# Last quarter of a squared-ReLU MLP: w_down's last 1,024 rows as a plain feature-major product instead of in seven products

## The chip, the cores and the metric

One core of one Trainium2 chip runs the whole decoder trunk (one layer, batch 1, 512 tokens, model width 1,024). The metric is the device time of one execution in microseconds, the median over repeated runs. Everything is in float32; the matmul operands are written as two float32r halves (a high half and the remainder), and each product is made of three matmuls.

## The reference, cut to what matters

```python
for i in range(DEPTH):                       # DEPTH = 1
    ...
    x = x + y @ w_out[i]                     # x1 in the kernel
    h2 = rms_norm(x, norm_mlp[i])
    x = x + jnp.square(jax.nn.relu(h2 @ w_up[i])) @ w_down[i]     # x2 in the kernel
    ple_gate = jax.nn.sigmoid(rms_norm(x, norm_ple[i]) @ w_ple_gate[i])
    x = x + ple_gate * (p[i] @ w_ple[i])
```

x is 512 x 1,024, w_up 1,024 x 4,096, w_down 4,096 x 1,024, w_ple_gate 1,024 x 1,024, p 512 x 256, w_ple 256 x 1,024. What comes ahead of `x @ w_out` (gated linear attention, block attention, their branches) is the same before and after the change.

## The kernel before, in words

**Layout.** Activations lie feature-major: 128 features on the partitions, 512 tokens along the free axis, 8 such tiles for the model width (KT = 8). A feature-major product (`gemm_fm`) takes one weight block of 1,024 x 128 (8 pieces of 128 x 128 as the stationary operand) and lets 128 x 512 tiles of the activation stream past; `mm3` issues the three matmuls of a pair of halves (lines 102, 103 and 104), so that one block is 24 matmuls of 512 columns into one of two PSUM banks ("acc").

**Order.** TensorE's order is written out by the program. `tick` is called twice per block: after 12 and after 24 matmuls. It first runs what was planned for this tick with `at(t, f)`, then advances small generators (`spawn`) by a step. A block's evacuation (`evac`) is issued behind its second tick, and what it spawns goes on with the next tick. Each engine then works through its own queue in this order and waits by semaphores.

**Weights.** A 512 KB weight block is loaded by SP's queue into one of three `raw` buffers 7 ticks ahead of its use (`unit`), and 3 ticks ahead `make` has it split: ScalarE writes the high half (`whi`, line 162), VectorE the remainder (`wlo`, line 164).

**The MLP.** It is cut into four quarters of 1,024 hidden features. In quarter g, eight blocks U0 to U7 form relu(h2 @ w_up) in feature-major tiles, which are then squared (`F`, slot a0). The product with w_down's 1,024 x 1,024 quarter is formed token-major by a scheme of seven half-size products P1 to P7 instead of eight (`quarter`): tokens, features and outputs are halved, sums and differences of `F` (GpSimd and VectorE) and of the weights (accumulating DMAs, `down_units`) are the operands, each product is 24 matmuls into two banks ("aux"), and `subtotal` and GpSimd add the results into `acc` (slot a6, 512 x 1,024, tokens on the partitions). The table `blocks` fixes the order: U0 to U3 of a quarter lie between the products of the quarter before, so that the last quarter has U4, U5, U6, P5, U7, P1, P2, P6, P7, P3, P4. `TP` is the tick at which the table ends.

**Turning back and the end.** `acc` is token-major and x2 is needed feature-major. `turn_back(i0)` transposes two feature tiles (four 128 x 128 transposes each, line 1012, into one bank), VectorE adds x1 to them (line 1018; x1 was written to DRAM as `spill` and is read back into slot a4 by `back_x1`), splits them for the next product (lines 97 and 98) and squares and sums them for the norm. Two of its four calls lie at the last two ticks of the table, two in the first p @ w_ple product (`gemm_ple(ple0)`: 4 tiles of 6 matmuls, evacuated by ScalarE in line 1078 from the two "acc" banks). Then come the norm's two matmuls (line 385), the eight gate blocks (`ple_gate`) and the other half of p @ w_ple (`ple1`, `ple_last`), which multiplies, adds and writes the result out.

```python
at(TP - 2, lambda: turn_back(0))
at(TP - 1, lambda: turn_back(2))
...
back = [4, 6]                    # gemm_ple: turn_back(back.pop(0)) behind every second tile
```

Of the kernel before, what the change touches and what calls it, by code (L numbers as in the profile page):

```python
# [21 lines left out]
F32 = mybir.dt.float32  # L22
# [22 lines left out]

@with_exitstack
def kernel(ctx: ExitStack, tc: tile.TileContext, xT, pT, w_in, w_val, w_glr, w2, cols,
                      w_a, w_b, w_out, w_up, w_down, w_gate, w_ple, outT):
    nc = tc.nc
    const = ctx.enter_context(tc.tile_pool(name="const", bufs=1))  # L50
    big = ctx.enter_context(tc.tile_pool(name="big", bufs=1))
# [9 lines left out]
    def nm(s):  # L61
        uid[0] += 1
        return f"{s}_{uid[0]}"
# [4 lines left out]
    def slot(tag, shape, dt=F32):  # L68
        return big.tile(shape, dt, tag=tag, name=nm(tag))
# [5 lines left out]
    def tt(tag, dt=F32):  # L75
        return tmp.tile([P, T], dt, tag=tag, name=nm(tag), bufs=BUFS.get(tag, 2))

    def bank(pool=auxp, tag="aux"):
        return pool.tile([P, T], F32, tag=tag, name=nm(tag))
# [37 lines left out]
    def at(t, f):  # L117

        plan.setdefault(t, []).append(f)
# [141 lines left out]
    def make(raw):  # L261
        hi = wp.tile([P] + list(raw.shape[1:]), F32R, tag="whi", name=nm("whi"))
        lo = wp.tile([P] + list(raw.shape[1:]), F32R, tag="wlo", name=nm("wlo"))
        ready.append((hi, lo))
        jobs.insert(0, [halves(hi, lo, raw), 0])

    blocks = [("U", 0, j) for j in range(4)]
    for g in range(4):  # L270
        mix = ["U4", "U5", "U6", "P5", "U7", "P1", "P2", "P6", "n0", "P7", "n1", "P3", "n2", "P4", "n3"]
        for z in mix:
            k = int(z[1])
            if z[0] != "n":
                blocks.append((z[0], g, k))
            elif g < 3:
                blocks.append(("U", g + 1, k))
    start = {z: T0 + 2 * j for j, z in enumerate(blocks)}
    TP = T0 + 2 * len(blocks)

    def down_units(g):


        c = {k: start["P", g, k] for k in range(1, 8)}
        box = {}

        def load(t, name, tag, u, src):
            def f():
                if name not in box:
                    box[name] = slot(tag, [P, 2, 512] if tag[0] == "v" else [P, 2, 2, 512])  # L290
                nc.sync.dma_start(out=of(name, u), in_=src)
            at(t, f)

        def of(name, u):
            return box[name] if name[0] == "S" else box[name][:, u]

        def add(t, name, u, src):
            at(t, lambda: G.dma_start(out=of(name, u), in_=src, accum_op=ALU.add))

        def use(k, name, u):  # L300
            at(c[k] + u - 3, lambda: make(of(name, u)))

        for u in range(2):
            a11, a12 = w_down[0, 4 * g + u], w_down[0, 4 * g + 2 + u]
            a21, a22 = w_down[1, 4 * g + u], w_down[1, 4 * g + 2 + u]
            t = c[5] + u
            S = f"S{u}"
            load(t - 10, S, f"v{u}", u, a22)
            load(t - 9, "A21", "c0", u, a21)
            load(t - 8, "A11", "c1", u, a11)  # L310
            load(t - 1, "A12", "c3", u, a12)
            load(c[1] + u, "A22", "c1", u, a22)
            add(t - 8, S, u, a21)
            add(t - 5, "A21", u, a11)
            add(t - 1, S, u, a11)
            if g < 3:
                add(c[6] + u - 1, S, u, a12)
            else:
                last_sum(t, u, (a22, a21, a11, a12))
            for k, name in ((5, S), (1, "A11"), (6, S), (2, "A12"), (7, "A21"), (3, S), (4, "A22")):  # L320
                if g < 3 or k != 3:
                    use(k, name, u)
                else:
                    at(c[3] + u - 3, lambda u=u: make(sums[u]))

    sums = {}

    def last_sum(t, u, srcs):

        def f():  # L330
            sums[u] = wp.tile([P, 2, 512], F32, tag="raw", name=nm("raw"))
            nc.sync.dma_start(out=sums[u], in_=srcs[0])
        at(start["U", 3, 7] + u - 6, f)
        for j in range(3):
            at(start["U", 3, 7] + u + 3 * j - 4, lambda j=j: G.dma_start(out=sums[u], in_=srcs[j + 1],
                                                                     accum_op=ALU.add))

    for g in range(4):
        for j in range(8):
            unit(start["U", g, j], w_up[8 * g + j, 0])  # L340
        down_units(g)
    unit(TP, w_ple[0])
    for j in range(8):
        unit(TP + 2 + 2 * j, w_gate[j, 0])
# [518 lines left out]

    acc = None
    h3 = []
    s2 = R2 = x2 = p_hl = None

    def subtotal(first, out, ps, op):

# [133 lines left out]

        return block

    def turn_back(i0):

        nonlocal s2, R2
        for i in range(i0, i0 + 2):
            ps = bank()  # L1010
            for m in range(NT):
                PE.transpose(ps[:, m * P:(m + 1) * P], acc[:, m, i * P:(i + 1) * P], ident)
            if not i:
                h3.append(slot("a5", [P, KT, T], F32R))
                h3.append(slot("a0", [P, KT, T], F32R))
                R2 = const.tile([P, T], F32, tag="R", name="R2")
                s2 = tt("s")
            V.tensor_tensor(x2[:, i], ps, x2[:, i], ALU.add)
            scaled_split(h3[0][:, i], h3[1][:, i], x2[:, i], col[:, C_PLE + i:C_PLE + i + 1])
            if i == 0:  # L1020
                A.activation(s2, x2[:, i], AF.Square)
            else:
                q = tt("q2")
                A.activation(q, x2[:, i], AF.Square)
                G.tensor_tensor(s2, s2, q, ALU.add)
            if i == KT - 1:
                spawn(norm_end(R2, s2), 1)

    def back_x1():
        nonlocal x2  # L1030
        x2 = slot("a4", [P, KT, T])
        nc.sync.dma_start(out=x2, in_=spill)

    def load_p():
        nonlocal p_hl
        raw = wp.tile([P, 2, T], F32, tag="raw", name=nm("raw"))
        nc.sync.dma_start(out=raw, in_=pT)
        yield 1
        p_hl = slot("c0", [P, 4, T], F32R)
        yield from halves(p_hl[:, :2], p_hl[:, 2:], raw)  # L1040

    at(start["P", 3, 1] + 1, back_x1)
    at(start["P", 3, 3], lambda: spawn(load_p()))
    at(TP - 2, lambda: turn_back(0))
    at(TP - 1, lambda: turn_back(2))
    quarters = {}
    for z, g, i in blocks:
        if g not in quarters:
            quarters[g] = quarter(g)
        quarters[g](z, i)  # L1050


    mid = slot("a1", [P, KT, T])

    back = [4, 6]

    def gemm_ple(evac, n=4):
        w = ready.pop(0)
        for i in range(n):
            ps = bank(accp, "acc")  # L1060
            ms = slice(i * P, (i + 1) * P)
            for k in range(2):
                mm3(ps, (w[0][:, k, ms], w[1][:, k, ms]), (p_hl[:, k], p_hl[:, 2 + k]), k == 0, k == 1)
            if i == 3:
                convert()
            if i % 2:
                if back:
                    turn_back(back.pop(0))
                tick()
            evac(i, ps)  # L1070
        return w

    def finish(i, e):
        V.tensor_tensor(e, e, x2[:, i], ALU.add)
        nc.sync.dma_start(out=outT[i * P:(i + 1) * P], in_=e)

    def ple0(i, ps):
# [1 line left out]

    def ple_gate(i, ps):  # L1080
        e = tt("e") if i < 4 else mid[:, i]
        if i < 2:
            A.activation(e, ps, AF.Copy)
        else:
            V.tensor_tensor(e, ps, R2, ALU.mult)
            A.activation(e, e, AF.Sigmoid)

        def rest():
            if i < 2:
                yield 2 - i  # L1090
                V.tensor_tensor(e, e, R2, ALU.mult)
                A.activation(e, e, AF.Sigmoid)
                yield 1
            V.tensor_tensor(e, e, mid[:, i], ALU.mult)
            finish(i, e)
            yield 1
        if i < 4:
            spawn(rest())

    def ple1(i, ps):  # L1100
        e = mid[:, 4 + i]
# [3 lines left out]
    def ple_last(w):  # L1105

        for c in range(2):
            s = slice(c * 256, (c + 1) * 256)
            ps = bank(accp, "acc")
            ms = slice(3 * P, 4 * P)  # L1110
            for k in range(2):
                mm3(ps[:, :256], (w[0][:, k, ms], w[1][:, k, ms]), (p_hl[:, k, s], p_hl[:, 2 + k, s]),
                    k == 0, k == 1)
            e = mid[:, KT - 1, s]
            V.tensor_tensor(e, e, ps[:, :256], ALU.mult)
            V.tensor_tensor(e, e, x2[:, KT - 1, s], ALU.add)
            nc.sync.dma_start(out=outT[(KT - 1) * P:, s], in_=e)

    gemm_ple(ple0)
# [66 lines left out]
```

## Time and profile before

| | us |
|---|---|
| median of 3 runs (lowest to highest) | 976.58 (975.85 to 977.4) |
| the profiled execution, its own time | 977.64 |
| its span, first to last instruction | 975.9 |
| TensorE busy (98% of the span) | 956.2 |
| VectorE busy (63%) | 619.1 |
| ScalarE busy (48%) | 470.1 |
| GpSimd busy (24%) | 232.3 |

How to read it: PE is TensorE, PEld its weight loads, DVE VectorE, ACT ScalarE, POOL GpSimd, SP the engine that issues most DMAs. A matmul's record is longer than the time until the next one starts, since matmuls are pipelined; what a matmul costs in a stream is the distance from start to start. The clock is TensorE's granted clock as a share of full speed (1.00 is 2.4 GHz, 0.50 is 1.2 GHz). The execution's own time is 1.7 us above its span.

### The profile page before, as it was taken

The page shows a single profiled execution, that of the slowest core. Times are in us where ns is not written, and L with a number is a line of the kernel's source. Part 1 is how long each engine was busy: PE and PEld are TensorE (multiplying, and loading weights), DVE is VectorE, ACT ScalarE, POOL GpSimd, SP SyncE. Part 2 cuts the span into 40 slices and gives each one's busy share as a digit, 9 for nine tenths or more (in the row PEclk, how much of TensorE's full clock was granted, in tenths as well). Part 3 has the DMA queues.
Part 4 walks back from the last instruction along what each step waited for, and adds up shares of the span by engine and source line. Part 5 has one row for each costly group of instructions (what it writes and reads, how often), then busy time and mean ns, then how long its engine had stood idle before and what let it go on. Part 6 is the DMA issues. An engine that isn't in the chain of part 4 may idle for free.

```text
span 975.9 us, 11466 instructions
## 1 busy us (share of the span) xinstructions
PE 956.2 (98%) x4360; PEld 791.7 (81%) x4360; DVE 619.1 (63%) x807; ACT 470.1 (48%) x691; POOL 232.3 (24%) x204
## 2 busy tenths in 40 slices
PE   9999999999999999999999999999999999999698
PEld 7888888878888888888888888788878878887486
DVE  5469989785556763333365555775695596589564
ACT  4558878774155842212323354624443353353551
POOL 0027674610321000000000004142153334335300
PEclk9999999999999999999999999999999999999799
DMA  7222121213211232343223459528635852994041
GB/s 259 86 87 66 64 77 46 74 58 108 87 65 45 74 121 87 108 150 130 87 99 109 139 183 269 134 83 242 189 88 175 215 149 79 310 276 133 22 151 43
DMA packets 34903, 121.15 MB, mean 124 GB/s; under 512 B 4000, under 2 KB 4384, under 8 KB 34464
## 3 DMA queue, kind: packets, MB, share of 16 engines
q1 hardware_dynamic: 29520, 101.53, 29.9%
q0 software_dynamic: 5184, 18.88, 10.1%
q8 instruction: 34, 0.56, 0.2%
q14 instruction: 21, 0.17, 0.0%
q10 hardware_dynamic: 144, 0.02, 0.0%
HBM read 116.21 MB, written 4.19 MB: 123 GB/s over the span
## 4 chain that ended last, share of the span: by engine, by line
PE 85%; DVE 9%; ACT 3%; issue 2%; POOL 0%; DVEq 0%; ACTq 0%; POOLq 0%
PE acc L102 22%; PE acc L104 22%; PE acc L103 22%; PE aux L103 5%; PE aux L104 5%; PE aux L102 5%; DVE wlo L164 3%; DVE a L164 2%; DVE a L871 1%; ACT whi L162 1%; PE aux L583 1%; PE aux L750 1%; PE aux L386 1%; PE aux L385 1%; PE aux L753 1%
## 5 line engine op out<-in xcount | busy, mean ns | idle before, releaser
L102 PE MATMUL acc<-a,whi 128*128 128x512 f32 x832 | 326.4, 392 | 0.0
L104 PE MATMUL acc<-a,wlo 128*128 128x512 f32 x832 | 324.5, 390 | 1.6 <-DVE wlo L164 1.6
L103 PE MATMUL acc<-a,whi 128*128 128x512 f32 x832 | 324.3, 390 | 0.0
L164 DVE TENSOR_TENSOR wlo<-raw,whi 128x1024 fp32r<-128x1024 f32 x130 | 172.7, 1331 | 95.8 <-ACT whi L162 94.6
L162 ACT ACTIVATE whi<-raw 128x1024 fp32r<-128x1024 f32 x130 | 136.4, 1050 | 108.1 <-PE acc L103 71.3
L104 PEld LDWEIGHTS acc<-a,wlo 128*128 128x128 f32 x832 | 156.3, 188 | 35.9 <-DVE wlo L164 2.8
L102 PEld LDWEIGHTS acc<-a,whi 128*128 128x128 f32 x832 | 156.5, 188 | 32.1
L103 PEld LDWEIGHTS acc<-a,whi 128*128 128x128 f32 x832 | 156.5, 188 | 31.8
L103 PE MATMUL aux<-wlo,a 128*128 128x512 f32 x288 | 112.3, 390 | 1.5 <-DVE wlo L164 1.5
L104 PE MATMUL aux<-whi,a 128*128 128x512 f32 x288 | 112.6, 391 | 0.0
L102 PE MATMUL aux<-whi,a 128*128 128x512 f32 x288 | 112.2, 390 | 0.0
L936 POOL TENSOR_TENSOR c<-a 128x256 f32<-128x256 f32 x16 | 14.1, 885 | 315.3 <-ACT a L925 315.3
L103 PEld LDWEIGHTS aux<-wlo,a 128*128 128x128 f32 x288 | 54.1, 188 | 13.6 <-DVE wlo L164 2.4
L104 PEld LDWEIGHTS aux<-whi,a 128*128 128x128 f32 x288 | 54.1, 188 | 12.6 <-DVE a L164 1.5
L102 PEld LDWEIGHTS aux<-whi,a 128*128 128x128 f32 x288 | 54.1, 188 | 11.1
L925 ACT ACTIVATE a<-a 128x512 f32<-128x512 f32 x32 | 20.1, 630 | 71.9 <-DVE a L917 68.6
L164 DVE TENSOR_TENSOR wlo<-c,whi 128x1024 fp32r<-128x1024 f32 x32 | 48.8, 1555 | 8.7 <-ACT whi L162 8.7
L162 ACT ACTIVATE whi<-c 128x1024 fp32r<-128x1024 f32 x32 | 33.7, 1055 | 31.4 <-PE acc L103 12.4
L513 POOL TENSOR_TENSOR ql<-q,qh 128x512 fp32r<-128x512 f32 x16 | 22.9, 1430 | 86.3 <-ACT qh L511 86.3
L102 PE MATMUL acc<-c,whi 128*128 128x512 f32 (+1 forms) x82 | 32.9, 402 | 7.2 <-ACT a L1078 7.1
L810 ACT ACTIVATE a<-a 128x512 f32<-128x512 f32 x16 | 10.1, 632 | 61.5 <-DVE a L809 61.5
L871 DVE TENSOR_TENSOR a<-a,aux 128x512 f32<-128x512 f32 x42 | 27.1, 681 | 17.0 <-PE aux L104 17.0
(211 smaller groups left out, 1362.0 us busy)
## 6 DMA issues: line engine op xcount, KB each, us to landing
raw<-in_w_in_dram SPq DMA_DIRECT2D x48, 512.0 KB, 3.2
raw<-in_w_up_dram SPq DMA_DIRECT2D x32, 512.0 KB, 3.7
c<-in_w_down_dram SPq DMA_DIRECT2D x32, 512.0 KB, 10.1
v<-in_w_down_dram POOLq DMA_DIRECT2D x22, 512.0 KB, 9.0
raw<-in_w_val_dram SPq DMA_DIRECT2D x14, 512.0 KB, 3.3
raw<-in_w_a_dram SPq DMA_DIRECT2D x8, 512.0 KB, 3.2
raw<-in_w_b_dram SPq DMA_DIRECT2D x8, 512.0 KB, 3.2
raw<-in_w_out_dram SPq DMA_DIRECT2D x8, 512.0 KB, 3.4
```

The lines of the kernel that those rows point to most:

```text
L102: PE.matmul(ps, a[0], b[0], start=start, stop=False)
L103: PE.matmul(ps, a[0], b[1], start=False, stop=False)
L104: PE.matmul(ps, a[1], b[0], start=False, stop=stop)
L162: A.activation(hi, src, AF.Copy)
L164: (eng or V).tensor_tensor(lo, src, f32(hi), ALU.subtract)
L385: PE.matmul(ps, ones[n], sh, start=True, stop=False)
L386: PE.matmul(ps, ones[n], sl, start=False, stop=True)
L513: G.tensor_tensor(sl, q2, f32(sh), ALU.subtract)
L810: A.activation(s, s, AF.Sigmoid)
L871: V.tensor_tensor(out, out, ps, op)
L925: A.activation(e, e, AF.Square)
L936: G.tensor_tensor(t1[:, k], F[:, 0, i], F[:, 1, i], ALU.subtract)
```

## The change

The last quarter's eight products of w_up are followed by eight blocks W0 to W7: a plain feature-major product of all 1,024 squared features with one 1,024 x 128 column block of w_down's last quarter, which the host lays out as `w_last`. The sums that the seven products needed (of features, of weights) disappear for this quarter, `last_sum` with them. `acc` now holds three quarters only; `turn_back(i)` transposes one tile of it at each of eight ticks, from the second tick of U5 to the first of W1, and adds it to x1, which `back_x1` now reads in two halves into slots c0 and c1. W i's evacuation adds its bank to that sum, which is x2, and splits, squares and sums it there. The features of the last quarter are split into halves of their own (`first_halves`, `last_up`, slots a1 and a2). `gemm_ple` has no transposes any more, and the norm's sum is formed on VectorE instead of GpSimd; the first two gates no longer wait for the norm in a generator of their own. Cut to what the prediction speaks of:

```diff
     blocks = [("U", 0, j) for j in range(4)]
-    for g in range(4):
+    for g in range(3):
         mix = ["U4", "U5", "U6", "P5", "U7", "P1", "P2", "P6", "n0", "P7", "n1", "P3", "n2", "P4", "n3"]
...
+    blocks += [("U", 3, j) for j in range(4, 8)] + [("W", 3, j) for j in range(8)]
...
-                last_sum(t, u, (a22, a21, a11, a12))
...
+    for j in range(8):
+        unit(start["W", 3, j], w_last[j, 0])
...
+    def back_x1():
+        for j in range(2):
+            x1b = slot(f"c{j}", [P, 4, T])
+            nc.sync.dma_start(out=x1b, in_=spill[:, 4 * j:4 * j + 4])
+            for i in range(4):
+                x2[4 * j + i] = x1b[:, i]
+    def turn_back(i):
+        ps = bank()
+        for m in range(NT):
+            PE.transpose(ps[:, m * P:(m + 1) * P], acc[:, m, i * P:(i + 1) * P], ident)
+        V.tensor_tensor(x2[i], ps, x2[i], ALU.add)
+    def first_halves(i):
+        if not ff:
+            ff.append(slot("a1", [P, KT, T], F32R))
+            ff.append(slot("a2", [P, KT, T], F32R))
+        yield from halves(*ff_of(i), f_first[:, i])
+    def last_up(i, ps):
+        nonlocal f_first
+        if i == 0:
+            f_first = slot("a0", [P, 4, T])
+        e = f_first[:, i] if i < 4 else tt("e")
+        V.scalar_tensor_tensor(e, ps, 0.0, R1, ALU.max, ALU.mult)
+        def rest():
+            A.activation(e, e, AF.Square)
+            if i >= 4:
+                yield from halves(*ff_of(i), e)
+        spawn(rest())
+    def last_down(i, ps):
+        V.tensor_tensor(x2[i], ps, x2[i], ALU.add)
+        if i == 0:
+            h3.append(slot("a4", [P, KT, T], F32R))
+            h3.append(slot("a5", [P, KT, T], F32R))
...
+        scaled_split(h3[0][:, i], h3[1][:, i], x2[i], col[:, C_PLE + i:C_PLE + i + 1])
+        add_square(s2, x2[i], i)
+        if i == KT - 1:
+            spawn(norm_end(R2, s2))
...
-    at(start["P", 3, 1] + 1, back_x1)
-    at(start["P", 3, 3], lambda: spawn(load_p()))
-    at(TP - 2, lambda: turn_back(0))
-    at(TP - 1, lambda: turn_back(2))
+    t = start["U", 3, 4]
+    at(t - 2, back_x1)
+    for i in range(4):
+        at(t + i, lambda i=i: spawn(first_halves(i)))
+    for i in range(KT):
+        at(t + 3 + i, lambda i=i: turn_back(i))
+    at(start["W", 3, 1], lambda: spawn(load_p()))
...
+        if z == "W":
+            gemm_fm(1, ff_of, lambda _, ps: last_down(i, ps))
+        elif g == 3:
+            gemm_fm(1, kt_of(h2_hi, h2_lo), lambda _, ps: last_up(i, ps))
...
-                if back:
-                    turn_back(back.pop(0))
                 tick()
...
-        "w_down": _rows(a["w_down"][0]),
+        "w_down": _rows(a["w_down"][0, :3 * D]),
+        "w_last": _columns(a["w_down"][0, 3 * D:]),
```

How the order of instructions stands at two places, on two engines. (A name's first part is its slot, or its pool's tag; the numbers count the tiles.) First TensorE. Before, in the first p @ w_ple product: the second tile's last three matmuls, eight transposes of `acc` (a6), the third tile's first matmul.

```order
L102 MATMUL acc_1146_6990<-c0_1128_6897,whi_1125_6892 128x512
L103 MATMUL acc_1146_6990<-c0_1128_6897,whi_1125_6892 128x512
L104 MATMUL acc_1146_6990<-c0_1128_6897,wlo_1126_6893 128x512
L1012 MATMUL aux_1147_6997<-ident_80,a6_806_4746 128x128 x4
L1012 MATMUL aux_1149_7008<-ident_80,a6_806_4746 128x128 x4
L102 MATMUL acc_1151_7020<-c0_1128_6897,whi_1125_6892 128x512
```

Now, at the seam of U7 and W0: U7's last three matmuls, the four transposes of tile 4, W0's first four matmuls on the squared features' halves (a1, a2).

```order
L102 MATMUL acc_1082_6607<-a4_737_4264,whi_1070_6543 128x512
L103 MATMUL acc_1082_6607<-a5_738_4265,whi_1070_6543 128x512
L104 MATMUL acc_1082_6607<-a4_737_4264,wlo_1071_6544 128x512
L1005 MATMUL aux_1087_6645<-ident_80,a6_806_4746 128x128 x4
L102 MATMUL acc_1089_6655<-a1_1063_6487,whi_1077_6593 128x512
L103 MATMUL acc_1089_6655<-a2_1064_6488,whi_1077_6593 128x512
L104 MATMUL acc_1089_6655<-a1_1063_6487,wlo_1078_6594 128x512
L102 MATMUL acc_1089_6655<-a1_1063_6487,whi_1077_6593 128x512
```

What moved: the transposes stand in groups of four inside the stream of w_up and W blocks, and none is left in the p @ w_ple product.

Second VectorE. Before, from the end of the seven products into the p @ w_ple product: the last additions to `acc` stand between the turned-back tiles' additions (L1018) and splits (L98).

```order
L1018 TENSOR_TENSOR a4_1099_6729<-aux_1131_6915,a4_1099_6729 128x512
L98 SCALAR_TENSOR_TENSOR a0_1133_6921<-a4_1099_6729,col_78,a5_1132_6920 128x512
L1018 TENSOR_TENSOR a4_1099_6729<-aux_1135_6928,a4_1099_6729 128x512
L98 SCALAR_TENSOR_TENSOR a0_1133_6921<-a4_1099_6729,col_78,a5_1132_6920 128x512
L871 TENSOR_TENSOR a6_806_4746<-a6_806_4746,aux_1129_6901 128x512
L871 TENSOR_TENSOR a6_806_4746<-a6_806_4746,aux_1130_6902 128x512
L1018 TENSOR_TENSOR a4_1099_6729<-aux_1140_6957,a4_1099_6729 128x512
L98 SCALAR_TENSOR_TENSOR a0_1133_6921<-a4_1099_6729,col_78,a5_1132_6920 128x512
L1018 TENSOR_TENSOR a4_1099_6729<-aux_1142_6968,a4_1099_6729 128x512
L98 SCALAR_TENSOR_TENSOR a0_1133_6921<-a4_1099_6729,col_78,a5_1132_6920 128x512
```

Now, around the seam of U7 and W0: L1022 evacuates an up block, L1006 adds a turned-back tile to x1, L164 into a2 is the lower half of a feature tile, into `wlo` that of a weight block.

```order
L1022 SCALAR_TENSOR_TENSOR e_1081_6605<-acc_1075_6559,R1_4266 128x512
L1006 TENSOR_TENSOR c0_1057_6450<-aux_1083_6620,c0_1057_6450 128x512
L164 TENSOR_TENSOR a2_1064_6488<-e_1081_6605,a1_1063_6487 128x512
L1006 TENSOR_TENSOR c1_1058_6452<-aux_1087_6645,c1_1058_6452 128x512
L164 TENSOR_TENSOR wlo_1085_6642<-raw_1072_6545,whi_1084_6641 128x1024
L1022 SCALAR_TENSOR_TENSOR e_1088_6653<-acc_1082_6607,R1_4266 128x512
L1006 TENSOR_TENSOR c1_1058_6452<-aux_1090_6668,c1_1058_6452 128x512
L164 TENSOR_TENSOR a2_1064_6488<-e_1088_6653,a1_1063_6487 128x512
L1006 TENSOR_TENSOR c1_1058_6452<-aux_1094_6693,c1_1058_6452 128x512
L164 TENSOR_TENSOR wlo_1092_6690<-raw_1079_6595,whi_1091_6689 128x1024
```

What moved: the eight turn-back additions are spread between the evacuations and weight splits of U5 to W1; the feature tile of U7 (the last L164 into a2) stands behind an addition that waits for the transposes of the middle of W0.

## Rows read from the trace of the kernel before

**Rows 1.** The page: the span, and TensorE's busy time.

```profile
span 975.9 us, 11466 instructions
PE 956.2 (98%) x4360; PEld 791.7 (81%) x4360; DVE 619.1 (63%) x807; ACT 470.1 (48%) x691; POOL 232.3 (24%) x204
```

**Rows 2.** Stretches from U4 of the last quarter to the end.

```profile
core 0: us, PE busy (x) PEld busy (x) DVE busy (x) ACT busy (x) POOL busy (x), PEclk, DMA share, GB/s
835.85:899.48 63.63, 61.84 (x274) 50.12 (x272) 50.41 (x47) 29.09 (x32) 28.29 (x24) 1.00 0.84 233
899.48:910.42 10.94, 5.08 (x29) 3.83 (x28) 7.07 (x11) 6.40 (x10) 3.85 (x3) 0.90 0.19 63
910.42:921.70 11.28, 8.64 (x24) 6.56 (x25) 4.82 (x7) 4.62 (x8) 2.53 (x2) 0.50 0.14 48
921.70:965.53 43.83, 43.71 (x192) 35.83 (x191) 23.74 (x30) 21.34 (x28) 2.59 (x2) 1.00 0.25 84
965.53:975.90 10.37, 5.92 (x31) 4.81 (x29) 6.29 (x11) 0.63 (x1) 0.00 (x0) 1.00 0.28 102
```

**Rows 3.** Timeline of TensorE: first matmuls of U4 and U5 (start, length).

```profile
835.85 0.39 PE L102 MATMUL acc<-a,whi 128*128 128x512 f32 x1
...
841.29 0.39 PE L102 MATMUL acc<-a,whi 128*128 128x512 f32 x1
```

**Rows 4.** Timeline of TensorE from the p @ w_ple product on.

```profile
904.38 0.33 PE L1012 MATMUL aux<-ident,a 128*128 128x128 f32 x1 [1.13 <-DVE a L871]
...
910.42 0.80 PE L102 MATMUL acc<-c,whi 128*128 128x512 f32 x1 [4.46 <-ACT a L1078]
...
911.44 0.63 PE L104 MATMUL acc<-c,wlo 128*128 128x512 f32 x1
911.87 0.63 PE L102 MATMUL acc<-c,whi 128*128 128x512 f32 x1
...
918.71 1.91 PE L1012 MATMUL aux<-ident,a 128*128 128x128 f32 x8
...
920.27 0.77 PE L102 MATMUL acc<-a,whi 128*128 128x512 f32 x1
```

**Rows 5.** TensorE's waits over the whole span: total us, times, longest.

```profile
PE acc L102 <- ACT a L1078: 7.1, 2, 4.5
```

**Rows 6.** Timeline of TensorE: four transposes inside a stream, early on.

```profile
45.18 0.60 PE L482 MATMUL aux<-ident,R 128*128 128x128 f32 x4
...
45.86 0.39 PE L103 MATMUL acc<-wlo,a 128*128 128x512 f32 x1
```

**Rows 7.** Stretch of the eight x1 blocks (w_out), columns as in Rows 2.

```profile
527.50:571.00 43.50, 43.50 (x194) 36.01 (x193) 25.80 (x32) 18.20 (x25) 0.00 (x0) 1.00 0.45 145
```

**Rows 8.** Groups from 835 us on, VectorE and ScalarE (busy, mean ns | idle).

```profile
L164 DVE TENSOR_TENSOR wlo<-raw,whi 128x1024 fp32r<-128x1024 f32 x14 | 19.4, 1393 | 10.6 <-ACT whi L162 10.6
L164 DVE TENSOR_TENSOR wlo<-c,whi 128x1024 fp32r<-128x1024 f32 x8 | 14.9, 1885 | 1.4 <-ACT whi L162 1.4
L1018 DVE TENSOR_TENSOR a<-aux,a 128x512 f32<-128x512 f32 x8 | 5.5, 683 | 4.1 <-PE aux L1012 4.1
L98 DVE SCALAR_TENSOR_TENSOR a<-a,col,a 128x512 fp32r<-128x512 f32 x8 | 6.0, 751 | 6.3 <-ACT a L97 6.3
...
L162 ACT ACTIVATE whi<-raw 128x1024 fp32r<-128x1024 f32 x14 | 14.7, 1049 | 10.3 <-DMA raw<-in_w_down_dram 4.8 <-PE acc L103 3.9 <-PE aux L104 1.7
L97 ACT ACTIVATE a<-a,col 128x512 fp32r<-128x512 f32 x8 | 5.8, 722 | 17.6 <-DVE a L1018 17.6
L1024 ACT ACTIVATE q<-a 128x512 f32<-128x512 f32 x7 | 4.3, 614 | 0.0
L1078 ACT ACTIVATE a<-acc 128x512 f32<-128x512 f32 x4 | 2.2, 578 | 0.0
```

**Rows 9.** DMA issues: KB each, median us from issue to landing.

```profile
a<-spill SPq DMA_DIRECT2D x1, 2048.0 KB, 16.6
```

**Rows 10.** Timeline of SP's queue: the load of U6's weights (quarter 3).

```profile
827.33 0.33 SPq L256 DMA_DIRECT2D raw<-in_w_up_dram  x1
```

## What the change will do to the time: the prediction

> **What bounds the kernel now.** I read the page first: TensorE is busy for 956.2 of 975.9 us [rows 1], so only its own work and the few places where it stands still can move the time. Next the stretches [rows 2], cut at U4 of the last quarter (835.85), at the end of the seven products (899.48) and at the second half of p @ w_ple (965.53). The first stretch is dense: 61.84 of 63.63 us. The next two are not: of 22.2 us TensorE works 13.7, and from 910.42 to 921.70 at a granted clock of 0.50, which is 1.2 GHz. The fourth is dense at 1.00, the last is the tail with the write-out. The timeline shows what happens in between [rows 4]: transposes wait for the last additions to the accumulator, then TensorE stands for 4.46 us until ScalarE has emptied a bank; behind that pause, matmuls start 0.43 us apart (911.44 to 911.87). The list of waits puts 7.1 us in two waits on that copy, its longest entry for TensorE [rows 5]. ScalarE and VectorE are not short of time on average there; the copies queue behind the splits and squares of turned-back tiles, each of which waits for VectorE.
>
> What one block costs in a dense stream: U4 starts at 835.85, U5 at 841.29 [rows 3], so 24 matmuls take 5.44 us, 0.227 each.
>
> **The change, part by part.** Everything ahead of 835.85 keeps its instructions on TensorE; in the four up blocks lying in the third quarter the other engines have less to do. I leave that time as it is.
>
> *From U4 to the end of w_down.* Before: 11 blocks in 63.63 us (59.84 of matmuls, the rest transposes and waits). After: 4 up blocks and 8 W blocks, 12 x 5.44 = 65.28. The plain product thus costs one block more, 24 matmuls. Sums of features on GpSimd and VectorE, accumulating DMAs and 14 weight tiles fall away; 8 of the same size replace these. None of it was on the path but for the waits that end with the stretch.
>
> *Transposes.* The same 32, now in eight groups of four inside the stream. Four of them in a stream early in the kernel start at 45.18, and the second matmul behind them at 45.86 [rows 6]: 0.68, less one matmul of 0.227, is 0.45 a group, 8 x 0.45 = 3.60. The Trainium skill says otherwise, in "TensorE: Matmul & The Clock Gate", Part 4: a transpose takes about 275 ns in a kernel and does not count as work for the clock. By that price, as an estimate, 32 would take 8.8 us and the sum would be 5.2 higher; the row, at a quarter to a third of it for each, decides for me.
>
> *What hides the new work of VectorE and ScalarE.* In U5, the fullest block, VectorE has one turn-back addition (0.68), one weight split (1.39), an evacuation (0.68, as the addition) and three lower halves of feature tiles (at most 0.68 each) [rows 8]: 4.8 of the 5.9 us that the block takes on TensorE. A W block has a weight split, an addition, a lower half (0.75) and a sum: 3.5 of 5.44. The x1 blocks earlier have the same work per tile, and there TensorE is busy for 43.50 of 43.50 us [rows 7]. If this cover went, the lateness of one block would show as a wait at the next block's weights, which are split one block ahead.
>
> *The seam of U7 and W0* is the tightest place. W0 needs U7's features for its last pair of pieces: high half 21 matmuls and a group of transposes after its start (4.77 + 0.45 = 5.2 us), lower half one matmul later (5.4). VectorE first adds tile 4 (done 0.85 us after W0's start), splits W1's weights (2.2), evacuates U7 (2.9); ScalarE squares (3.5) and copies the high half (4.1). The lower half stands on VectorE behind tile 5's addition, which waits for transposes in the middle of W0 (3.3, done at 4.0), and is ready at 4.8. So 0.6 us to spare, and I charge nothing. With the weight split at the 1.885 us that the same form takes beside a busy GpSimd [rows 8] it would still just do.
>
> *x1 read back.* Two loads of 1 MB now stand on SP's queue directly behind U6's weights, issued at 827.33 [rows 10]. The one load of 2 MB took 16.6 us to land [rows 9]; at that price x1 is there at 844.4, and the first addition needs it after U5, at 835.85 + 10.88 + 0.36 = 847.1. U7's weights are queued behind and are split only after U5 too. No charge.
>
> *The first p @ w_ple product* loses its transposes, splits and squares: 24 matmuls, 5.44 us. What is left is W7's evacuation. From W7's end: addition 0.68, ScalarE's high half 0.72, square 0.61, first copy 0.58 [rows 8], together 2.6 where the third tile wants the bank at 2.7; VectorE's lower half and sum end at 2.8, ScalarE's half of the norm's sum at 3.5, the second copy at 4.1, where the fourth tile wants it at 4.1. With hand-overs that is a wait of 0 to 1 us; I take 0.5, far below the 4.46 after which the clock was at 0.50.
>
> *The rest.* The norm's two matmuls 0.45, eight gate blocks 43.52, and the tail as it is, 10.37 [rows 2].
>
> **Sum.** 65.28 + 3.60 + 5.44 + 0.5 + 0.45 + 43.52 + 10.37 = 129.16 against 140.05 from 835.85 to 975.90: 10.9 less. Made of two parts: 68.9 instead of 63.6 up to the end of w_down (5.3 more), 49.9 instead of 66.05 from there to 965.53 (16.1 less). The profiled execution's own 977.64 becomes 966.7; it was 1.06 above the median of 976.58, so the median becomes **965.7 us**. Bounds of the charges: transposes 0.36 a group (0.7 less), no wait at p @ w_ple (0.5 less) or 1 us (0.5 more), and the runs before spread 0.8 to either side.
>
> **Rivals.**
>
> *A. Many short waits* in the stretch of turn-backs (U5 to W1), because an addition at the head of VectorE's queue waits for transposes that stand behind 12 matmuls, and weights and features queue behind it. For it: the margin of 0.6 us at W0, and hand-overs not in my sum. Against: margins of a block elsewhere. At 0.4 us for each of eight groups it is 3.2 us: 968.9.
>
> *B. The pause stays at p @ w_ple.* ScalarE's copies still stand in one queue with W7's half, square and the norm's half. If they are late by 3 us and the clock falls as before, the 24 matmuls behind cost 0.2 more each: 3 - 0.5 + 4.9 = 7.4 more, 973.1. Against it: six splits and squares of tiles are gone from that queue.
>
> *C. Transposes are dearer inside the stream*, as they are at 1.2 GHz, where eight took 1.56 us [rows 4], 0.78 a group. With that for all groups it is 2.6 us more, 968.3. By the price of the Trainium skill above, as an estimate, it would be 970.9.
>
> *D. Slower: the clock falls in the stretch of turn-backs.* From U5 to W1 a group of transposes follows every 12 matmuls. If those gaps and short waits took the clock to 1.2 GHz there, 96 matmuls at 0.43 instead of 0.227 would cost 19.5 us and 32 transposes 2.6: 987.8. The change loses as soon as more than (10.9 + 2) / 0.203 = 64 matmuls run so. Against: the clock was 1.00 in the first stretch although TensorE stood for 1.8 of its 63.63 us [rows 2], and behind the transposes inside a stream [rows 6] matmuls went on at full pace. The rule of the Trainium skill in the same section of "TensorE: Matmul & The Clock Gate", that transposes do not count as work for the clock, speaks for D; no row here shows it at work.
>
> *E. It comes to nothing*, if the waits just move: the plain product's 5.44 us are certain, so 16 us of pauses would all have to return. I see no place for them.
>
> **How the numbers follow.** Forecast 0.70, A 0.15, B 0.05, C 0.05, D 0.03, E 0.02. About 0.2%, 2 us, is what a measurement of this kernel can tell from no change. Faster: forecast, A, B and C, 0.95; within it: E, 0.02; slower: D, 0.03. The range goes from 965.7 - 0.7 - 0.5 - 0.8 = 963.7 up to A and C with the spread, 969.7; B, D and E lie outside.
>
> **What would show it.** In the trace after: no wait on ScalarE over 1 us in the first p @ w_ple product; granted clock 1.00 from U4 to the tail; about 0.45 us for each group of transposes; W0 to W7 at 5.44 us each, the first two a group longer; U4 to the end of w_down in 69 us, from there to the second half of p @ w_ple in 50. It is wrong if TensorE waits on VectorE's lower halves at W0 or on the reload of x1, or if the clock drops anywhere past U4.

## The result, and the profile after

| | before | after |
|---|---|---|
| median (lowest to highest), us | 976.9 (975.85 to 977.4) | 966.61 (966.41 to 966.75) |
| the profiled execution, its own time | 977.64 | 966.75 |
| its span | 975.9 | 965.0 |

The ratio of the two is 0.9896, 95% interval 0.9879 to 0.9913: 10.3 us faster. (The median before is of four runs here, of three in the table ahead of the prediction.) Run again, the changed kernel took 966.73 us beside 977.21, ratio 0.9892 (0.9875 to 0.9908).

The page after the change answers to [rows 1]: 24 more matmuls, 10.9 us less span, and TensorE at 99%.

```profile
span 965.0 us, 11441 instructions
PE 955.7 (99%) x4384; PEld 793.2 (82%) x4384; DVE 597.7 (62%) x799; ACT 459.5 (48%) x682; POOL 188.2 (20%) x168
```

The stretches, columns as in [rows 2], cut at U4, at the end of W7's matmuls, after the norm's matmuls and at the second half of p @ w_ple:

```profile
835.85:904.94 69.09, 69.09 (x321) 57.17 (x320) 42.66 (x54) 28.83 (x40) 0.00 (x0) 1.00 0.30 103
904.94:911.30 6.36, 6.36 (x29) 4.85 (x28) 3.19 (x6) 4.74 (x8) 0.00 (x0) 1.00 0.23 82
911.30:954.80 43.50, 43.50 (x194) 36.01 (x193) 21.05 (x26) 17.13 (x21) 0.00 (x0) 1.00 0.25 85
954.80:965.00 10.20, 5.88 (x31) 4.78 (x29) 6.29 (x11) 0.63 (x1) 0.00 (x0) 0.88 0.28 103
```

In the first three rows TensorE's busy time equals the length of the stretch and the clock is 1.00. From U4 to the end of w_down the changed kernel takes 69.09 us where the old one took 63.63, and the 10.94 + 11.28 us of the old second and third stretch have become 6.36. In the last row the clock is below 1.00 only over the write-out: TensorE's last matmul ends at 960.83, the clock is 1.00 up to 962.00 and 0.65 on average from there to 963.50.

The timeline of TensorE through the first p @ w_ple product answers to [rows 4]. Around its third and fourth tile some 0.3 us are lost, and gate 0 starts at 911.22 instead of 920.27:

```profile
905.01 0.39 PE L102 MATMUL acc<-c,whi 128*128 128x512 f32 x1
...
907.73 0.48 PE L102 MATMUL acc<-c,whi 128*128 128x512 f32 x1
908.05 0.40 PE L103 MATMUL acc<-c,whi 128*128 128x512 f32 x1
...
909.25 0.50 PE L102 MATMUL acc<-c,whi 128*128 128x512 f32 x1
909.59 0.39 PE L103 MATMUL acc<-c,whi 128*128 128x512 f32 x1
...
910.75 0.40 PE L368 MATMUL aux<-qh,ones 128*128 128x512 f32 x1
...
911.22 0.40 PE L102 MATMUL acc<-a,whi 128*128 128x512 f32 x1
```

ScalarE in the same place: W7's high half (L97), its square, the first copy out of a bank (L1091, line 1078 before), the norm's half (L92) and the other copies. The first copy, for which TensorE had stood 4.46 us, now ends at 907.67; the third tile wants the bank at 907.73, twelve matmuls after 905.01:

```profile
905.94 0.72 ACT L97 ACTIVATE a<-c,col 128x512 fp32r<-128x512 f32 x1 [2.30 <-DVE c L1032]
906.57 0.62 ACT L398 ACTIVATE q<-c 128x512 f32<-128x512 f32 x1
907.09 0.58 ACT L1091 ACTIVATE a<-acc 128x512 f32<-128x512 f32 x1
908.08 0.63 ACT L92 ACTIVATE qh<-s 128x512 fp32r<-128x512 f32 x1 [0.42 <-DVE s L399]
908.62 0.58 ACT L1091 ACTIVATE a<-acc 128x512 f32<-128x512 f32 x1
```

The seam of U7 and W0 on VectorE: W1's weight split, U7's evacuation, tile 5's addition with its wait for the transposes, the lower half of feature tile 7. W0's first matmul starts at 859.91.

```profile
860.80 1.22 DVE L164 TENSOR_TENSOR wlo<-raw,whi 128x1024 fp32r<-128x1024 f32 x1
861.94 0.69 DVE L1022 SCALAR_TENSOR_TENSOR e<-acc,R 128x512 f32<-128x512 f32 x1
863.41 0.69 DVE L1006 TENSOR_TENSOR c<-aux,c 128x512 f32<-128x512 f32 x1 [0.79 <-PE aux L1005]
864.02 0.68 DVE L164 TENSOR_TENSOR a<-e,a 128x512 fp32r<-128x512 f32 x1
```

It ends at 864.70, W0 + 4.8, and TensorE's first matmul on it starts at 865.51, 0.8 us later: no wait is there.

### The profile page after: what moved, and what is told of

Same layout as the page of the kernel before. It is cut to its first block, busy times and chain, and to the rows that moved or that the text cites. A ratio compares the mean times of both kernels' runs of the same rounds, so it can differ in the third digit from the quotient of the medians.

```text
span 965.0 us, 11441 instructions
## 1 busy us (share of the span) xinstructions
PE 955.7 (99%) x4384; PEld 793.2 (82%) x4384; DVE 597.7 (62%) x799; ACT 459.5 (48%) x682; POOL 188.2 (20%) x168
## 4 chain that ended last, share of the span: by engine, by line
PE 90%; DVE 5%; ACT 2%; issue 1%; DMA 1%; SPq 0%; DVEq 0%; ACTq 0%
PE acc L104 24%; PE acc L102 24%; PE acc L103 24%; PE aux L103 5%; PE aux L104 4%; PE aux L102 4%; DVE wlo L164 1%; DVE a L164 1%; PE aux L566 1%; PE aux L733 1%; ACT whi L162 1%; DMA a<-in_xT_dram 1%; DVE a L854 1%; PE aux L368 1%; PE aux L736 1%
## 5 line engine op out<-in xcount | busy, mean ns | idle before, releaser
L102 PE MATMUL acc<-a,whi 128*128 128x512 f32 x896 | 351.6, 392 | 0.0
L104 PE MATMUL acc<-a,wlo 128*128 128x512 f32 x896 | 349.2, 390 | 1.6 <-DVE wlo L164 1.6
L103 PE MATMUL acc<-a,whi 128*128 128x512 f32 x896 | 349.1, 390 | 0.0
L164 DVE TENSOR_TENSOR wlo<-raw,whi 128x1024 fp32r<-128x1024 f32 x136 | 176.3, 1298 | 91.3 <-ACT whi L162 89.3
L104 PEld LDWEIGHTS acc<-a,wlo 128*128 128x128 f32 x896 | 168.2, 188 | 38.2 <-DVE wlo L164 2.8
L102 PEld LDWEIGHTS acc<-a,whi 128*128 128x128 f32 x896 | 168.3, 188 | 34.4
L103 PEld LDWEIGHTS acc<-a,whi 128*128 128x128 f32 x896 | 168.3, 188 | 34.1
L104 PE MATMUL aux<-whi,a 128*128 128x512 f32 x232 | 90.6, 391 | 0.0
L103 PE MATMUL aux<-wlo,a 128*128 128x512 f32 x232 | 90.3, 389 | 0.0
L102 PE MATMUL aux<-whi,a 128*128 128x512 f32 x232 | 90.3, 389 | 0.0
L104 PEld LDWEIGHTS aux<-whi,a 128*128 128x128 f32 x232 | 43.5, 188 | 10.2 <-DVE a L164 1.2
L102 PEld LDWEIGHTS aux<-whi,a 128*128 128x128 f32 x232 | 43.6, 188 | 9.0
L164 DVE TENSOR_TENSOR wlo<-c,whi 128x1024 fp32r<-128x1024 f32 x24 | 34.0, 1448 | 7.2 <-ACT whi L162 7.2
L97 ACT ACTIVATE a<-c,col 128x512 fp32r<-128x512 f32 x16 | 11.6, 723 | 50.6 <-DVE c L829 25.9
L379 DVE SCALAR_TENSOR_TENSOR w<-aux,w 128x512 f32<-128x512 f32 x23 | 15.9, 691 | 28.5 <-ACT w L377 28.5
```

Of the source, the lines that this page charges most:

```text
L97: A.activation(hi, x, AF.Copy, scale=g)
L102: PE.matmul(ps, a[0], b[0], start=start, stop=False)
L103: PE.matmul(ps, a[0], b[1], start=False, stop=False)
L104: PE.matmul(ps, a[1], b[0], start=False, stop=stop)
L164: (eng or V).tensor_tensor(lo, src, f32(hi), ALU.subtract)
L379: V.scalar_tensor_tensor(w, ps, EPS, w, ALU.add, ALU.mult)
```

## The experiments

Theory: the gain is **cover**. In the kernel before, turning a tile back is a chain over VectorE and ScalarE with nothing for TensorE to do meanwhile; in the changed one the same work lies beside W blocks. Rivals: the gain is the plain product as such (no sums, no accumulating DMAs); it is the clock alone, at 0.50 behind the pause; or the pause is a matter of the two banks, to be had for less. Each was run beside the kernel before, whose medians were 976.4 to 977.2 us.

**late_turn: the plain product, turned back at the end.** The changed kernel, but the turning back, splits and squares stand where they stood before, and with them the norm's sum (on GpSimd) and the first two gates' evacuations. The main lines:

```diff
-    for i in range(KT):
-        at(t + 3 + i, lambda i=i: turn_back(i))
+    at(TP - 2, lambda: turn_back(0))
+    at(TP - 1, lambda: turn_back(2))
...
+                if back:
+                    turn_back(back.pop(0))
```

> The plain product of the last quarter stays; turning the other quarters' sum back, its splits and squares go back to where they were before (two calls in the last two ticks, two in the first p @ w_ple product). My theory (the gain is the cover that the up and W blocks give to turning back, the plain product itself costs 5.4 us): most of the pause returns, shorter than before since the sum is complete early and VectorE has no products to evacuate: pauses and half clock of 4 to 10 us at p @ w_ple, 971 to 977 us. Rival (the plain product is itself the gain, through the sums, accumulating DMAs and weight splits that it spares): 968 or less.

Measured: 979.34 us (978.7 to 981.37), ratio 1.0026 (1.0017 to 1.0035): above the range that I had given, slower even than the kernel before, and 12.7 us slower than the changed one (979.34 - 966.61). TensorE's longest waits in the stretch at the end (total us, times, longest):

```profile
PE acc L102 <- ACT a L1101: 5.7, 2, 4.0
PE acc L102 <- ACT c L162: 1.1, 1, 1.1
PE acc L103 <- DVE c L164: 1.0, 1, 1.0
```

The pause at p @ w_ple is back (4.0 us, line 1101 is the copy), and the half clock with it:

```profile
911.05 0.80 PE L102 MATMUL acc<-c,whi 128*128 128x512 f32 x1 [4.02 <-ACT a L1101]
911.65 0.63 PE L103 MATMUL acc<-c,whi 128*128 128x512 f32 x1
912.07 0.63 PE L104 MATMUL acc<-c,wlo 128*128 128x512 f32 x1
912.50 0.63 PE L102 MATMUL acc<-c,whi 128*128 128x512 f32 x1
```

The pause now comes ahead of the second tile, one earlier than before. The other two waits in the list, 2.1 us together, are for p's halves, which ScalarE and VectorE reach late among the turned-back tiles; I had not counted them, and without them the run would lie near the kernel before. VectorE also comes to W7's evacuation only behind four turned-back tiles, although W7's last matmul started at 901.71:

```profile
911.99 0.68 DVE L1047 TENSOR_TENSOR c<-acc,c 128x512 f32<-128x512 f32 x1
```

So late_turn does more than take the cover away: it also makes p's halves and W7's evacuation late, and how much of the time is due to the latter was not separated. What it shows is that the plain product without the cover brings nothing: the gain hangs on where the turning back stands.

**filler: TensorE kept busy in the pauses.** The kernel before with 20 and 18 matmuls of a constant, read by nothing, ahead of the third and fourth p @ w_ple tile.

```diff
+    n_fill = [0, 0, 20, 18]
...
         for i in range(n):
+            fill(n_fill.pop(0) if n_fill else 0)
             ps = bank(accp, "acc")
```

> The kernel before with 20 and 18 matmuls of ones against ones, 128x512, into a bank that nobody reads, put ahead of the third and fourth tile of the first p @ w_ple product, to fill the two pauses. My theory (the pause is set by VectorE and ScalarE, the half clock behind it is only a part of the loss): granted clock 1.00 there, the third tile still starts at about 910 us, and 1.5 to 3.5 us are saved: 973 to 975.5. Rival (the clock is the loss): the 24 matmuls at 0.43 us give back 4.9 us or more, 972 or less. Third (the filler just takes longer than the pause): 977 or more.

Measured: 976.15 us (975.18 to 976.8), ratio 0.9989 (0.9979 to 0.9998): a miss, 0.65 above my range and in neither of the others. The clock stays at 1.00, and the kernel gains 1.0 us (0.2 to 2.1 by the interval).

```profile
906.18 4.82 PE L1063 MATMUL aux<-ones 128*128 128x512 f32 x20
...
910.27 0.58 ACT L1088 ACTIVATE a<-acc 128x512 f32<-128x512 f32 x1
...
910.90 0.50 PE L102 MATMUL acc<-c,whi 128*128 128x512 f32 x1
911.23 0.40 PE L103 MATMUL acc<-c,whi 128*128 128x512 f32 x1
...
917.98 1.04 PE L1012 MATMUL aux<-ident,a 128*128 128x128 f32 x8
918.77 0.47 PE L102 MATMUL acc<-a,whi 128*128 128x512 f32 x1
...
924.88 0.50 PE L385 MATMUL aux<-qh,ones 128*128 128x512 f32 x1 [0.39 <-ACT qh L92]
925.90 0.50 PE L386 MATMUL aux<-ql,ones 128*128 128x512 f32 x1 [0.53 <-DVE ql L93]
```

Its matmuls run at full pace (0.23 us apart behind 911.23), and the third tile starts as ScalarE's copy ends (910.27 + 0.58 = 910.85): it is still the copy that decides, and the fillers delay nothing there. Gate 0 starts at 918.77 instead of 920.27, and two waits for the norm's halves (0.39 and 0.53 us) take part of that back. The expectation's 4.9 us counted 24 matmuls at half clock. In the kernel before it was 15 matmuls (the last two tiles' twelve and gate 0's first three), 0.2 us more each, and the eight transposes from 918.71 on [rows 4], 1.56 us where they take 0.79 here: 3.8 us. Of these 1.0 came back. Most of the half clock lay over time in which TensorE would have waited anyway; it was little of the loss.

**triple: three times the transposes.** The changed kernel with every turn-back transpose issued three times into the same place, 64 more.

```diff
-        for m in range(NT):
+        for m in list(range(NT)) * 3:
```

> The changed kernel with each turn-back's four transposes issued three times into the same bank: 64 transposes more in the stretch from U5 to W1. By the price in the stream (0.36 us for four): 16 x 0.36 = 5.8 us more, 972.4, clock 1.00. Rival C (0.78 us for four): 979. By the 275 ns that the Trainium skill's page "TensorE: Matmul & The Clock Gate", Part 4, gives for one, as an estimate: 984. Rival D (transposes are no work for the clock): the granted clock falls in that stretch, 985 or more.

Measured: 973.88 us (973.46 to 973.99), 7.2 us over the changed kernel (973.88 - 966.73), ratio 0.9964 (0.9951 to 0.9977) to the kernel before. TensorE's timeline at the first group, then the stretch from U4 to 911.00, near the end of w_down:

```profile
846.70 1.47 PE L1005 MATMUL aux<-ident,a 128*128 128x128 f32 x12
847.92 0.48 PE L102 MATMUL acc<-a,whi 128*128 128x512 f32 x1
848.24 0.40 PE L103 MATMUL acc<-a,whi 128*128 128x512 f32 x1
```

```profile
835.85:911.00 75.15, 75.15 (x381) 63.31 (x380) 41.66 (x54) 28.83 (x40) 0.00 (x0) 1.00 0.26 93
```

That is 1.5 us more than expected: a transpose costs 7.2 / 64 = 0.11 us, where the expectation had 0.09, and the clock is 1.00 although twelve of them stand behind every 12 matmuls. Rivals C (dear transposes) and D (the clock falls there) are both refuted, with three times the dose.

**lag, banks, lagbanks: small repairs of the pause.** On the kernel before: *lag* issues a turned-back tile's lower half behind the next tile's addition, so that VectorE does not stand idle until ScalarE has the high half; *banks* takes the first p @ w_ple tiles from the "aux" banks; *lagbanks* does both.

```diff
-            scaled_split(h3[0][:, i], h3[1][:, i], x2[:, i], col[:, C_PLE + i:C_PLE + i + 1])
+            A.activation(h3[0][:, i], x2[:, i], AF.Copy, scale=col[:, C_PLE + i:C_PLE + i + 1])
+            low_half()
+            lag.append(i)
...
```

```diff
-            ps = bank(accp, "acc")
+            ps = bank() if n == 4 else bank(accp, "acc")
```

> The kernel before with one edit: in turning back, VectorE's lower half of a tile is issued behind the next tile's addition, so that VectorE does not wait for ScalarE's high half (0.8 us idle in each tile before). If that round trip of the two engines is what makes the pauses: 8 x 0.7 to 0.8 = 6 us off the chain, 971 to 974. Rival (the bank that ScalarE's copies empty late, or the transposes' place in TensorE's queue): 975.5 or more.

> The kernel before with one edit: the first p @ w_ple product's four tiles go to the six aux banks instead of the two acc banks, so that the third tile need not wait for ScalarE's copy of the first. If the bank is the cause: both waits (7.1 us) and the half clock (4.9 us) go, 966 to 969. If the chain of VectorE and ScalarE over eight tiles is the cause, the wait moves to the first gate's feature tiles and only the late transposes of the last two tiles are won: 971 to 975.

> The kernel before with both small edits, the lagging lower half and the aux banks for the first p @ w_ple product. If each took away its own part of one chain, they add: 977.2 - 4 - 2 = 971. If the clock too stays up, because no pause is long any more, 3 to 5 us on top: 966 to 968. If the tiles' chain on VectorE and ScalarE is then still longer than its cover: 972 or more.

Measured: lag 973.23 us, ratio 0.9955 (0.994 to 0.9969); banks 975.21, 0.9977 (0.9968 to 0.9987); lagbanks 971.49, 0.9941 (0.9926 to 0.9956). Lag lies in the range expected, banks and lagbanks 0.2 and 0.5 us above theirs. They add up to 5 to 6 us, half of what the change brings. With lag the wait on the copies is still the first of TensorE's list; with banks it moves to the transposes and the norm:

```profile
PE acc L102 <- ACT a L1089: 5.8, 2, 3.6
```

```profile
PE aux L385 <- ACT qh L92: 1.1, 1, 1.1
PE aux L1012 <- ACT a L1078: 1.1, 1, 1.1
PE aux L1012 <- DVE a L871: 1.0, 3, 0.5
PE aux L1012 <- DVE a L1018: 1.0, 1, 1.0
```

So the bank that TensorE waited for was the last link of a chain, not its cause: take it away, and the link before it shows. The clock still fell to half in all three (0.50 from 908 to 916 us in lag, 914 to 916 in banks, 918 to 920 in lagbanks).

**cover7, cover7b, cover7c, cover7d: cover without the plain product.** If cover is the gain, it should be had with the seven products too, 24 matmuls (5.44 us) cheaper. Both halves of p @ w_ple (E0, E1) are moved into the end of the seven products, one between P3 and P4, one behind P4, and the tiles are turned back one at a time beside them. The run also has lag's lower half and banks' "aux" banks, and its last gate is formed in two column halves. Of its edit, the order of blocks:

```diff
             elif g < 3:
                 blocks.append(("U", g + 1, k))
+            elif k == 2:
+                blocks.append(("E", 3, 0))
+    blocks.append(("E", 3, 1))
...
```

> The kernel before with its seven products kept in the last quarter too; both halves of p @ w_ple are used as cover for turning back, one between P3 and P4, one behind P4, the tile of one call at a time, VectorE's lower half of a tile issued behind the next tile's addition; p is loaded earlier, and the last gate is done in two column halves. My theory: cover is what counts and 24 matmuls less are worth 5.4 us, less a longer tail and some waits for VectorE in P7 to P4: 961 to 966. Rival (only the plain product relieves VectorE enough): pauses stay behind P4, 970 or more.

Measured: 973.93 us (973.65 to 976.36), ratio 0.997 (0.9961 to 0.998). TensorE's longest wait is for p's lower half, which stands in VectorE's queue behind the weight splits of the products:

```profile
PE aux L103 <- DVE c L164: 6.2, 1, 6.2
```

In *cover7b* p is loaded at P5 through a weight buffer, in *cover7c* eight ticks ahead of P5 into two free tiles, and the weight splits of P4 and E1 go ahead of a turned-back tile's work (against cover7, the main lines):

```diff
-        raw = slot("c2", [P, 2, T])
-        nc.sync.dma_start(out=raw, in_=pT)
-        yield 3
+        raw = [tt("e"), tt("e")]
+        for k in range(2):
+            nc.sync.dma_start(out=raw[k], in_=pT[:, k])
+        yield 9
...
```

> cover7 with p loaded and split during P5 and U7 (into slot c2) instead of behind P7, where TensorE waited 6.2 us for the lower half of p in VectorE's queue and lost the clock. My theory (seven products can be kept, cover is what counts): 6.2 us of wait and about 2.6 us of half clock go, 962 to 966, level with or below the changed kernel. Rival (VectorE is the bound from P1 to P4, the work of the seven products just makes the next thing late): 968 or more.

> cover7b with p loaded straight into two evacuation tiles that are free then, so that no weight buffer is taken from the stream (cover7b waited 2.4 us at P1 for it and then ran 5 us at half clock), and with the weight splits of P4 and of the second half of p @ w_ple issued ahead of a turned-back tile's work. My theory: those 2.4 + 2.6 us and about 2 us of waits around P4 go, 962 to 965, at or below the changed kernel. Rival (VectorE, full from P1 to P4, gives each gain back at the next product): 967 or more.

Measured: cover7b 970.87 us, ratio 0.9933 (0.9918 to 0.9948), with the wait moved to P1 (2.4 us on ScalarE's feature halves, then half clock until 877.6); cover7c 968.03, 0.9903 (0.9888 to 0.9918), the clock at 1.00 to the end. All three missed my range, and each lies in its rival's. In *cover7d* E1's turned-back tiles stand ahead of the weight split and the first gate takes the lower halves last:

> cover7c with the last waits taken on: in the second half of p @ w_ple the turned-back tiles stand ahead of the weight split of the second gate, and the first gate's last four pieces use the features' lower halves last. My theory: the 2.1 us that TensorE waited there for lower halves go, 965 to 966.5, level with the changed kernel or 1 us below it; with seven products the waits for VectorE between P1 and P4 (2 to 3 us) stay. Rival (those waits reappear at the norm or at the second gate): 967.5 or more.

The changed kernel itself was run once more beside these:

> The changed kernel once more, on the chip and beside the runs of the two above, for a comparison with cover7c: 966.6 again.

Measured: 966.73 us for the changed kernel. cover7d: 967.17 us (966.56 to 967.37), ratio 0.9901 (0.9885 to 0.9918): level with the changed kernel, not better, and between the two ranges expected. TensorE's waits, and two stretches around P1 to P4:

```profile
PE aux L388 <- ACT qh L92: 1.3, 1, 1.3
PE aux L104 <- DVE wlo L164: 0.9, 1, 0.9
PE aux L102 <- DVE a L1028: 0.8, 1, 0.8
PE aux L103 <- DVE wlo L164: 0.5, 1, 0.5
PE aux L389 <- DVE ql L93: 0.5, 1, 0.5
```

```profile
870.00:880.00 10.00, 10.00 (x46) 8.27 (x45) 10.00 (x11) 6.53 (x8) 4.17 (x3) 1.00 1.04 338
880.00:890.00 10.00, 9.47 (x41) 7.21 (x40) 6.92 (x8) 4.56 (x5) 2.54 (x2) 1.00 0.67 185
```

The waits make 4.0 us, four of the five on VectorE (2.7 us), which is busy for 10.00 of 10.00 us from 870 to 880 with the sums and splits that the seven products need. Against the changed kernel 5.44 us of matmuls are saved and the span is 0.6 us longer, so 6.0 us came back: these 4.0, some 1.7 in matmuls beside the waits and transposes, which follow each other more slowly than the 0.227 us of a dense stream, and 0.4 from the last matmul's start to the end (4.85 us instead of 4.45).

So with cover the seven products and the plain product take the same time, and without it neither is faster than the kernel before. That carries the theory: cover is the gain, and the plain product is one way to it, not a condition. Of cover7d's 9.3 us, though, lag's and banks' edits bring 5.7 by themselves (lagbanks); the rest came with the cover. Whether a further reordering would get ahead was not tried; no run beat the changed kernel.

## Why the prediction was right

The forecast was 965.7 us, in 963.7 to 969.7, faster with 0.95; measured 966.61. From U4 to the end the span holds 129.15 us, where the sum had 129.16. That the two agree to 0.01 us is luck: the terms are off by up to 0.2 us, and cancel. Term by term:

- **The plain product and the transposes**: 68.9 forecast, 69.09 measured from 835.85 to 904.94. U5's first group of transposes starts at 846.75, that is 835.85 + 10.90; a group costs 0.35 us to the next matmul and 0.09 more for that one, 0.44 where 0.45 was charged. late_turn shows that this product is a cost and not the gain.
- **Cover**: from there to 954.80 forecast 49.9, measured 6.36 + 43.50 = 49.86. late_turn keeps the plain product and gives up the cover, and 12.7 us return (2.1 of them waits for p's halves).
- **The seam of U7 and W0**: the lower half was forecast for W0 + 4.8 and was ready at W0 + 4.8. Two parts differ and cancel: W1's weight split took 1.22 instead of 1.39, and VectorE stood idle for 0.79 ahead of tile 5's addition, as the transposes decide that moment. To spare was 0.8 us, not 0.6.
- **The first p @ w_ple product**: I took 0.5 us of waiting; the stream took 905.01 to 910.75, 5.74, so 0.3 over 24 matmuls.
- **The tail**: 10.37 forecast, 10.20 measured from 954.80 to 965.00.
- **x1 read back**: at the price of the one 2 MB load I had it there by 844.4 (the sum's own terms, 827.33 and 16.6, give 843.9). The two loads landed in 6.7 us each (median), some 10 us ahead of the first addition at 847. No charge, as forecast, with the bound far off.

```profile
c<-spill SPq DMA_DIRECT2D x2, 1024.0 KB, 6.7
```

- **From the profile to the median**: the one step that was off. I took the profiled execution's distance to the median before (977.64 against 976.58, 1.06) for the changed kernel as well. Its profiled execution was forecast at 966.7 and took 966.75; its median lies only 0.14 below that. The 0.9 us between forecast and median is this step: in the comparisons the kernel before had a median of 976.4 to 977.2, so 976.58 was on the low side.

**Rivals.** A (short waits in the turn-back stretch): none, TensorE was busy for 69.09 of 69.09 us. B (the pause stays): gone; late_turn shows that it stays when the turning back does, which fits the argument of the six splits and squares fewer in ScalarE's queue; but late_turn brings back more than these, and no run tests them alone. Its 24 matmuls at half clock were a misreading, 15 ran so in the kernel before. C and D: refuted by triple. The Trainium skill's 275 ns for a transpose ("TensorE: Matmul & The Clock Gate", Part 4) is for bf16; the mean length of a float32 transpose's record here, 272 ns, is near it, but that is not what one costs in a stream:

```profile
L1005 PE MATMUL aux<-ident,a 128*128 128x128 f32 x32 | 4.8, 272 | 0.0
```

The prediction put its row at a quarter to a third of that price; with 0.36 to 0.45 us for four it is a third to two fifths. No run here shows a clock that fell over transposes, at 4 or at 12 behind 12 matmuls. E: nothing came back in the changed kernel; late_turn comes nearest to it.

What the prediction did not see is how much of the old loss was the chain and how little the clock. Rival B priced the half clock at 4.9 us; filler gave the clock back in full, and 1.0 us came of it.

## What to carry to other kernels

A pause on the busiest engine that ends in a wait for a small copy is best read back to the chain that fed the copy: moving the whole chain beside dense work brought 10.3 us here, repairing single links 2 or 4 (both together 5.7), and filling the gap 1. It can pay to give up saved matmuls for it, as long as the block that is paid (5.4 us) is smaller than the pause that it covers (16 us); but it was not necessary: cover7d kept the saving and came within 0.6 us. There the sums and splits of the scheme that saves matmuls kept VectorE busy, and half of what was saved (2.7 of 5.4 us) went into waits for VectorE. A low clock beside a pause is not a cost of its own until a run with the clock held up shows how much comes back.

## What the runs showed that I had not expected

- Holding the clock at 1.00 through the old pauses was worth 1.0 us (filler), though 15 matmuls and eight transposes had run at half pace.
- The same weight split on VectorE (128 x 1,024) took 1.22 us on average in the changed kernel from U4 on, and 1.39 and 1.89 before [rows 8]; GpSimd, busy for 28.29 us of the old stretch [rows 2], is idle in the new one. The trace of the kernel before bears the connection out: all 149 splits of this size (weights or features) during which GpSimd computed nothing took 1.21 to 1.23 us, and the 64 during which it did took 1.20 to 3.90, 1.85 on average. No run took GpSimd's work away by itself.

```profile
L164 DVE TENSOR_TENSOR wlo<-raw,whi 128x1024 fp32r<-128x1024 f32 x20 | 24.4, 1222 | 5.8 <-ACT whi L162 5.1
```

- The plain product with the turning back left at the end is slower than the seven products (late_turn, 2.2 us beside the kernel before), although it has none of their sums; the waits for p's halves make 2.1 of the 2.2.
